# Sparse attention: the gate over the row sum goes through device memory and comes back as rows for 64 partitions a head, instead of being spread, transposed and copied

## The chip, the cores and the metric

The kernel runs on one core of one Trainium2 chip. The metric is the device time of one execution in microseconds (us); lower is better. The time of the kernel before is the median of three runs.

## What is computed

Two transformer-like blocks are computed for one sequence of 512 tokens and a model width of 1024, in float32. The change lies in the second layer of the second block, in its sparse attention with 16 query heads of width 64 over 4 key/value heads. Every query token attends in three branches, and a gate per token, head and branch weighs them:

```python
p_cmp = masked_softmax(s, ...)                      # branch 0: 32 compressed blocks
o_cmp = einsum("bhgqc,bchd->bqhgd", p_cmp, v_cmp)
...
p = masked_softmax(s, (tok <= t) ...)               # branch 1: selected blocks
o_sel = einsum("bhgqnk,bhqnkd->bqhgd", p, vs)
...
p = masked_softmax(s, wmask, axis=-1)               # branch 2: window
o_win = einsum("bhgqk,bkhd->bqhgd", p, vw)
o = g[..., 0:1] * o_cmp + g[..., 1:2] * o_sel + g[..., 2:3] * o_win
```

With 512 tokens the selection takes all blocks and the window reaches over all of the past, so branches 1 and 2 are both causal attention over 512 keys, with their own keys and values. The softmax is not divided before the product with the values: `exp` leaves the row sums, and the product is scaled afterwards by gate/sum. The change is about how this factor gets from its place to where the product needs it.

## The kernel before, in words

Tokens lie in four tiles of 128 (`NT` = 4, index `i`). The weights stream through SyncE's queue and are split in a high and a low part for TensorE; most of the time goes into matrix products with 512 columns (lines 474 to 476).

The attention stage is not written in program order. Every piece of work is added to a `Board` as a step with an engine letter (P = TensorE, S = ScalarE, V = VectorE, G = GpSimd, N = none), a cost in us, the steps it comes after, a rank, and what it takes and gives back of buffers. `Board.order` plays these steps through in time: the step that can begin first goes first, equal ones by rank. The order that comes out is the order in which the instructions are issued, each engine in its own order. A step on N holds no engine in this plan; it only lets its cost pass before its successors may begin.

There are 32 items `n` = (`pr`, `br`, `hh`): 8 pairs of heads, 2 branches, 2 heads. Two items that differ only in the head make one `m` = `n` // 2, 16 in all. For every item:

- SC (`at_s`, lines 2294 to 2296): scores of the four token tiles into three banks of PSUM on TensorE.
- MX (`at_m`, line 2306): row maxima on VectorE.
- EX (`at_x`, line 2322): `exp` on ScalarE, which also leaves the row sums in the small tile `asm`, 128 tokens x (4 tiles x 2 heads).
- TR (`at_t`, line 2349) and TH (`at_h`, line 381): transposes of the `exp` results on TensorE, and copies of them on ScalarE or VectorE.

For every `m`:

- GA (`at_g`): the reciprocal of the sums on VectorE (line 2331), and one product with the gates on GpSimd (line 2334), which spreads the 8 factors of a token over 512 columns (tile x head x 64) of a tile `u`.
- DT (`at_d`, line 2341): four transposes of `u` on TensorE into a bank, so that the 64 partitions of a head all carry its factors and the 512 tokens lie along the columns.
- DC (`at_e`, line 381 with `u`): a copy of that bank back into `u`, on ScalarE or VectorE.
- PV (`at_v`, line 2381): the product with the values on TensorE, 16 matmuls.
- U (`at_u`, line 2396): the product of PV's bank with `u`, on VectorE. It comes after DC and PV.
- For the second branch: PW (line 2388, the compressed branch), UC (line 2399), UA (line 2403), OH (line 381 with `oT`) and OL (line 2415), which add the three branches and split the sum for the output projection (steps D, lines 474 to 476 with `oT`).

GpSimd also has in this stage: the rotary steps QR (lines 1955 to 1958), some products of the compressed branch (line 2243), and at its end four loads of `h` from device memory (line 2505). The queries are turned for the scores by steps ST (line 2176). Elsewhere GpSimd's queue issues the DMAs of lines 1357 (`acsd`, 64 rows of 2 KB out of SBUF into device memory) and 1434 (`selh`, 32 runs of 512 bytes back out of `acsd`). The DMAs of lines 1881 to 1885 (`pe`, `w`, `rope`: 128 rows of 128 bytes, 1 KB and 512 bytes) are issued by ScalarE's queue.

Of the kernel before, what the change touches and what calls it, by code (L numbers as in the profile page):

```python
# [12 lines left out]
F32 = mybir.dt.float32  # L13
# [3 lines left out]
ALU = mybir.AluOpType  # L17
AX = mybir.AxisListType

P = 128  # L20
T = 512
D = 1024
NT = 4
# [317 lines left out]
def kernel(ctx: ExitStack, tc: tile.TileContext, ins, out):  # L341
    nc = tc.nc
    mm = nc.tensor.matmul
    V, S, G = nc.vector, nc.scalar, nc.gpsimd
# [11 lines left out]
    def nm(s):  # L356
        uid[0] += 1
        return f"{s}_{uid[0]}"
# [4 lines left out]
    def st(shape=(P, 512), dt=F32, name="s"):  # L363
        return bp.tile(list(shape), dt, name=nm(name), tag="s", bufs=NS)

    def bank(name="b"):
        return pp.tile([P, 512], F32, name=nm(name), tag="b", bufs=8)
# [12 lines left out]
    def copy(eng, o, a):  # L380
        S.copy(o, a) if eng == "S" else V.tensor_copy(o, a)
# [11 lines left out]
    ident = cp.tile([P, P], F32, name="ident")  # L393
# [266 lines left out]

    h = [None] * NT
    hsp = tc.dram_tile([T, D], F32, name="hsp")
    modc = cp.tile([P, 112], F32, name="modc")
    modp = [None]
    crow = cp.tile([P, D], F32, name="crow")
# [152 lines left out]
    for q in range(4):  # L818
        r = wp.tile([P, 1024], F32, name=f"xraw{q}", tag="raw", bufs=NRAW)
# [745 lines left out]
    kts = [None] * 16  # L1565
# [135 lines left out]
    for g in range(4):  # L1701
        steps = scan_steps(g)
        if g:
            q = Gr[g - 1]
# [21 lines left out]
    q = Gr[3]  # L1726
# [17 lines left out]
    kts = None  # L1744
# [226 lines left out]
    gts = kbg[:, 128:].rearrange("p (t j) -> p t j", t=NT)  # L1971
# [26 lines left out]
    B = Board(spare=ASPARE, slack=ASLACK)  # L1998
    qt = [gt(name="q") for _ in range(NT)]
    xk, Kx, Qs, wq, qb, qc, cb, pc, pcT = [], {}, {}, {}, {}, {}, {}, {}, {}  # L2000
    sb, nx, px, tb, pt, ob, db, us, sums, kts = {}, {}, {}, {}, {}, {}, {}, {}, {}, [None] * 8
    items = [(pr, hh, br) for pr in range(8) for br in range(2) for hh in range(2)]
    held = ws.n_split - ws.at
    loaded = ws.n_dma - ws.at
# [119 lines left out]
    for qr in range(4):  # L2124
        for t in range(NT):
            r = -5 if qr == 0 else QRANK[0] + QRANK[1] * (4 * qr - 4 + t)
            B.add(("Q", qr, t), "P", 2.57, lambda qr=qr, t=t: q_mm(qr, t),
                  (need(3) if qr < 2 else ["GM"] + need(8)) + ([("Q", qr, t - 1)] if t else [("Q", qr - 1, 3)] if qr else []),
                  r, take=1, give={"wh": 4, "wl": 4} if qr % 2 and t == 3 else ())
# [33 lines left out]
    for gp in range(2):  # L2163
        for br in range(2):
            r = KRANK if gp == 0 else 9 + br
            B.add(("KT", br, gp), "P", 0.44, lambda br=br, gp=gp: k_turn(br, gp), x_done + [("SC", 8 + 2 * br, 2)] if gp else [], r, take=1, short=True,
                  give={"s": 4} if gp and br else ())
# [24 lines left out]
    for pr in range(8):  # L2192
        r = 4 * pr - 3.5 if pr > 1 else -6
# [4 lines left out]
              give={"g": 4} if pr == 7 else ())  # L2198
# [60 lines left out]
    for hf in range(2):  # L2259
        r = -1 + 14 * hf  # L2260
        for tp in range(2):
            for qr in (2 * hf, 2 * hf + 1):
# [4 lines left out]
                      take={"s": 1} if qr % 2 == 0 else ())  # L2267
# [4 lines left out]
        for q in range(2):  # L2272
            B.add(("CT", hf, q), "P", 0.44, lambda hf=hf, q=q: c_turn(hf, q),
                  [("CX", hf, 0), ("CX", hf, 1)] + ([("CT", hf, 0)] if q else []), r, take=1, short=True,
                  give={"s": 2} if q else ())
# [7 lines left out]
    def at_s(n, q):  # L2283

        pr, hh, br = items[n]
        K = Kx[br, 2 * (pr // 4) + hh]
        qs = Qs[pr][:, hh]
        b = sb[n, q] = bank()
        at = 0
        for i in A_GRP[q]:  # L2290
            w = (i + 1) * P
            tl = slice(i * P, (i + 1) * P)
            o = b[:, at:at + w]
            mm(o, qs[:, tl], K[:, 1, :w], start=True, stop=False)  # L2294
            mm(o, qs[:, tl], K[:, 0, :w], start=False, stop=False)  # L2295
            mm(b[:, at + w - P:at + w], identb, camask, start=False, stop=True)  # L2296
            at += w

    def at_m(n, q):

        if n not in nx:
            nx[n] = small(4, "amx", 4)
        at = 0
        for i in A_GRP[q]:
            w = (i + 1) * P
            V.tensor_reduce(nx[n][:, i:i + 1], sb[n, q][:, at:at + w], AX.X, ALU.max, negate=True)
            at += w

    def at_x(n, q):

        if n not in px:
            if n % 2 == 0:
                sums[n // 2] = small(8, "asm", 4).rearrange("p (i h) -> p i h", h=2)
            px[n] = {}, gt(name="p"), st((P, 256), name="p")
        tiles, big, little = px[n]
        sm = sums[n // 2][:, :, n % 2]
        p = big[:, q * 512:(q + 1) * 512] if q < 2 else little
        b = sb.pop((n, q))
        at = 0
        for i in A_GRP[q]:  # L2320
            w = (i + 1) * P
            S.activation(p[:, at:at + w], b[:, at:at + w], AF.Exp, bias=nx[n][:, i:i + 1], accum_out=sm[:, i:i + 1])
            tiles[i] = p[:, at:at + w]
            at += w

    def at_g(m):

        pr, _, br = items[2 * m]
        nx.pop(2 * m), nx.pop(2 * m + 1)
        sm = sums.pop(m)  # L2330
        V.reciprocal(sm, sm)
        us[m] = st(name="u")
        gate = gts[:, :, 6 * pr:6 * pr + 6].rearrange("p i (h b) -> p i h b", b=3)[:, :, :, 1 + br:2 + br]
        G.tensor_tensor(us[m].rearrange("p (i h d) -> p i h d", i=NT, h=2), sm.unsqueeze(3).to_broadcast([P, NT, 2, 64]),
                        gate.to_broadcast([P, NT, 2, 64]), ALU.mult)

    def at_d(m):

        b = db[m] = bank()
        for i in range(NT):  # L2340
            nc.tensor.transpose(b[:, i * P:(i + 1) * P], us[m][:, i * P:(i + 1) * P], ident)

    def at_t(n, q):

# [22 lines left out]
    def KIND(n):  # L2367

        return ("raw" if items[n][1] else "wh"), ("raw" if n < NEARLY else "wl")
# [18 lines left out]
            mm(o[hh * 64:hh * 64 + 64], VB[:, pr // 4, 2 * (pr % 2) + hh], pcT[pr // 4][:, pr // 2 % 2],  # L2388
               start=True, stop=True)

    def at_e(m, eng):
        copy(eng, us[m], db.pop(m))

    def at_u(m):

        V.tensor_tensor(us[m], ob.pop(m), us[m], ALU.mult)
# [20 lines left out]
    for n, (pr, hh, br) in enumerate(items):  # L2417
        r, m = n, n // 2
        for q in range(3):
            B.add(("SC", n, q), "P", (0.52, 0.6, 0.32)[q], lambda n=n, q=q: at_s(n, q),  # L2420
                  [("SL", pr), ("K", br, pr // 4)], r + SCR, take=1,
                  give={"g": 1} if n in (3, 7) and q == 2 else {"g": 4} if n == 15 and q == 2 else ())
            B.add(("MX", n, q), "V", (0.62, 0.77, 0.37)[q], lambda n=n, q=q: at_m(n, q), [("SC", n, q)], r + MXR)
            B.add(("EX", n, q), "S", (0.87, 1.25, 0.62)[q], lambda n=n, q=q: at_x(n, q),
                  [("MX", n, q)] + ([("EX", n, 0)] if q else ["GS"]), r + EXR, take={"px": 1} if q == 0 else (), give=1)
        if hh:
            B.add(("GA", m), "G", 2.0, lambda m=m: at_g(m), [("EX", n - k, q) for k in range(2) for q in range(3)] + ["GC"],
                  r + 0.4, take={"s": 1})
        kinds = {KIND(n)[0]: 1}
        if hh == 0:  # L2430
            kinds[KIND(n)[1]] = kinds.get(KIND(n)[1], 0) + 1
        for q in range(3):
            d = [("EX", n, k) for k in range(3)]
            B.add(("TR", n, q), "P", (0.45, 0.34, 0.34)[q], lambda n=n, q=q: at_t(n, q),
                  d + ([("TR", n, q - 1)] if q else []), r - 1, take={"b": 1, **kinds} if q == 0 else 1, short=True,
                  give={"px": 1} if q == 2 else ())
            B.add(("TH", n, q), "SV", ((0.6, 0.5, 0.5)[q], (0.69, 0.56, 0.56)[q]), lambda eng, n=n, q=q: at_h(n, q, eng),
                  [("TR", n, q)] + ([("TH", n, q - 1)] if q else []) + ([("TH", n - 1, 2)] if q == 2 and hh else []),
                  r + 0.1, give=1)
        if hh:  # L2440
            back = dict(wh=1)
            for k in ("raw", KIND(n)[1]):
                back[k] = back.get(k, 0) + 1
            B.add(("PV", m), "P", 2.3, lambda m=m: at_v(m), [("TH", n - k, q) for k in range(2) for q in range(3)], r - 1,
                  take=1, short=True, give=back)
            B.add(("DT", m), "P", 0.5, lambda m=m: at_d(m), [("GA", m)], r - 0.5, take=1, short=True)
            B.add(("DC", m), "SV", (0.6, 0.69), lambda eng, m=m: at_e(m, eng), [("DT", m)], r, give=1)
            B.add(("U", m), "V", 0.72, lambda m=m: at_u(m), [("DC", m), ("PV", m)], r, give=1)
            if br:
                B.add(("PW", pr), "P", 0.9, lambda pr=pr: at_w(pr), [("U", m - 1), ("CH", pr // 4, pr // 2 % 2), "vc"],  # L2450
                      r - 1.5, take=1, short=True, give={"wl": 1} if pr == 3 else ())
                B.add(("UC", pr), "V", 0.69, lambda pr=pr: at_c(pr), [("PW", pr)], r - 0.5, give=1)
                B.add(("UA", pr), "GV", (1.3, 0.62), lambda eng, pr=pr: at_a(pr, eng), [("UC", pr), ("U", m)], r, give={"s": 1})
                B.add(("OH", pr), "SVG", (0.6, 0.4, 1.3), lambda eng, pr=pr: at_o(pr, eng), [("UA", pr)], r, take={"g": 1})
                B.add(("OL", pr), "GV", (1.3, 0.62), lambda eng, pr=pr: at_p(pr, eng), [("OH", pr)], r, give={"s": 1})
# [17 lines left out]
    for hf in range(2):  # L2473
        B.add(("gp", hf), "V", 1.6, lambda hf=hf: gr_prep(hf), [("GA", 11)] + ([("gc", 0)] if hf else []), 45,
              take={"s": 2, "g": 1 - hf})
# [22 lines left out]
    sb = tb = qt = B = None  # L2498
# [10 lines left out]
    kts = None  # L2509
# [100 lines left out]
```

## Time and profile before

| | |
|---|---|
| median of 3 runs | 2333.89 us (2333.24 to 2336.09) |
| the profiled execution's own time | 2337.24 us |
| its span in the trace | 2335.5 us |
| TensorE busy | 2271.2 us, 97% of the span |
| VectorE busy | 1444.5 us, 62% |
| ScalarE busy | 996.1 us, 43% |
| GpSimd busy | 209.3 us, 9% |
| packets under 512 bytes | 12424 of 98113 |

Busy time is summed over all instructions of an engine. A busy TensorE is not one at its peak, because the ends of its matmuls are modelled. The items of the attention run from about 1740 to 1925 us after the span's start; within that stretch the shares of the engines differ from those of the whole span.

### The profile page before, as it was taken

To read this page: it belongs to the slowest core of one execution; us is meant where nothing else is said; L and a number is where in the kernel's file an instruction comes from. 1 tells how busy PE (TensorE), PEld (TensorE's weight loads), DVE (VectorE), ACT (ScalarE), POOL (GpSimd) and SP (SyncE) were. 2 spreads that over 40 slices of the span, in tenths; PEclk is the share of its full clock that TensorE was granted. 3 is DMA by queue.
4 is the path that set the end of the run, shared out by engine and by line. 5 is a ranking of instruction groups with operands and counts; after the bars stand their busy time and mean duration, and the time that the engine had idled before them with its cause. 6 is when DMAs were issued, how large, how long until landed. Compare 5 with 4: busy or idle time off the path is not lost.

```text
span 2335.5 us, 30687 instructions
## 1 busy us (share of the span) xinstructions
PE 2271.2 (97%) x11890; PEld 1869.8 (80%) x11890; DVE 1444.5 (62%) x2411; ACT 996.1 (43%) x1697; POOL 209.3 (9%) x288
## 2 busy tenths in 40 slices
PE   8898999999999999999999999999999999999998
PEld 6676888788888887887789888888887768888887
DVE  3676666687855686776866556566757876323334
ACT  3454434342433365555535323236445765223122
POOL 0000040220000030110100000003332110000000
PEclk9998999999999999999999999999999999999999
DMA  5765523345642422221262567463420022323222
GB/s 177 201 182 149 184 87 118 126 135 193 191 148 90 130 90 76 73 76 61 74 230 88 193 191 239 147 209 106 130 55 10 19 100 91 108 73 109 90 90 72
DMA packets 98113, 286.75 MB, mean 123 GB/s; under 512 B 12424, under 2 KB 13192, under 8 KB 97968
## 3 DMA queue, kind: packets, MB, share of 16 engines
q1 hardware_dynamic: 59328, 209.02, 28.2%
q10 hardware_dynamic: 36288, 71.32, 9.2%
q0 software_dynamic: 2352, 4.46, 0.6%
q8 instruction: 93, 1.52, 0.3%
q14 instruction: 52, 0.43, 0.1%
HBM read 261.55 MB, written 8.52 MB: 116 GB/s over the span
## 4 chain that ended last, share of the span: by engine, by line
PE 73%; DVE 4%; ACT 1%; issue 1%; DMA 0%; POOL 0%; DVEq 0%; POOLq 0%; ACTq 0%
PE b L474 21%; PE b L476 21%; PE b L475 21%; PE b L2381 2%; PE b L2349 1%; PE b L2294 1%; PE b L2295 1%; PE b L1509 1%; PE b L1513 1%; DVE wl L157 0%; PE b L626 0%; DVE wl L115 0%; PE b L1474 0%; PE b L2388 0%; PE b L2296 0%
## 5 line engine op out<-in xcount | busy, mean ns | idle before, releaser
L474 PE MATMUL b<-xTl,wh 128*128 128x512 f32 (+1 forms) x1776 | 664.7, 374 | 9.5 <-DVE xTl L642 9.3
L476 PE MATMUL b<-xTh,wl 128*128 128x512 f32 (+1 forms) x1776 | 654.3, 368 | 0.5 <-DVE wl L115 0.5
L475 PE MATMUL b<-xTh,wh 128*128 128x512 f32 (+1 forms) x1776 | 654.1, 368 | 0.0
L115 DVE TENSOR_TENSOR wl<-raw,wh 128x1024 fp32r<-128x1024 f32 x317 | 388.0, 1235 | 287.2 <-ACT wh L114 286.2
L474 PEld LDWEIGHTS b<-xTl,wh 128*128 128x128 f32 x1776 | 336.8, 190 | 67.1 <-DVE xTl L642 11.6
L114 ACT CAST wh<-raw 128x1024 fp32r<-128x1024 f32 x317 | 327.3, 1049 | 142.1 <-PE b L476 66.9
L476 PEld LDWEIGHTS b<-xTh,wl 128*128 128x128 f32 x1776 | 335.9, 189 | 57.1 <-DVE wl L115 1.0
L475 PEld LDWEIGHTS b<-xTh,wh 128*128 128x128 f32 x1776 | 336.6, 190 | 54.3 <-issue 1.4
L474 PE MATMUL b<-wl,pT 128*128 128x512 f32 x520 | 202.7, 390 | 0.0
L476 PE MATMUL b<-wh,pT 128*128 128x512 f32 x520 | 202.3, 389 | 0.0
L475 PE MATMUL b<-wh,pT 128*128 128x512 f32 x520 | 202.3, 389 | 0.0
L706 DVE SCALAR_TENSOR_TENSOR mraw<-mraw,crow 128x512 f32<-128x512 f32 x224 | 145.6, 686 | 7.6 <-DMA mraw<-in_w_mod_dram 7.5
L474 PE MATMUL b<-wl,xTh 128*128 128x512 f32 (+1 forms) x352 | 127.8, 363 | 11.7 <-DVE wl L131 7.6
L476 PE MATMUL b<-wh,xTl 128*128 128x512 f32 (+1 forms) x352 | 124.8, 355 | 0.0
L475 PE MATMUL b<-wh,xTh 128*128 128x512 f32 (+1 forms) x352 | 124.7, 354 | 0.0
L476 PEld LDWEIGHTS b<-wh,pT 128*128 128x128 f32 x520 | 97.6, 188 | 20.2
L475 PEld LDWEIGHTS b<-wh,pT 128*128 128x128 f32 x520 | 97.6, 188 | 20.2
L474 PEld LDWEIGHTS b<-wl,pT 128*128 128x128 f32 x520 | 97.6, 188 | 20.1
L480 ACT CAST pT<-sa 128x512 fp32r<-128x512 f32 x44 | 27.3, 621 | 193.0 <-DVE sa L1753 193.0
L1169 ACT ACTIVATE c<-b,cols 128x512 f32<-128x512 f32 x44 | 34.4, 781 | 165.2 <-PE b L476 161.8
L1749 ACT ACTIVATE sa<-b 128x512 f32<-128x512 f32 x44 | 26.3, 598 | 162.1 <-PE b L476 159.0
L1753 DVE TENSOR_TENSOR sa<-sa,b 128x512 f32<-128x512 f32 x44 | 30.3, 688 | 88.4 <-PE b L476 88.4
(456 smaller groups left out, 3581.4 us busy)
## 6 DMA issues: line engine op xcount, KB each, us to landing
mraw<-in_w_mod_dram ACTq DMA_DIRECT2D x224, 256.0 KB, 3.7
raw<-in_w_f1u_dram SPq DMA_DIRECT2D x44, 512.0 KB, 3.7
raw<-in_w_f2u_dram SPq DMA_DIRECT2D x44, 512.0 KB, 3.7
raw<-in_w_f3u_dram SPq DMA_DIRECT2D x44, 512.0 KB, 3.7
raw<-in_w_f1d_dram SPq DMA_DIRECT2D x22, 512.0 KB, 3.6
raw<-in_w_f2d_dram SPq DMA_DIRECT2D x22, 512.0 KB, 3.6
raw<-in_w_f3d_dram SPq DMA_DIRECT2D x22, 512.0 KB, 3.6
raw<-in_w_sbqk_dram SPq DMA_DIRECT2D x16, 512.0 KB, 4.8
```

The lines of the kernel that those rows point to most:

```text
L114: self.nc.scalar.copy(h[:, :w], t[:, :w])
L115: self.nc.vector.tensor_sub(l[:, :w], t[:, :w], h[:, :w].bitcast(F32))
L474: mm(o, lh, rl, start=start, stop=False)
L475: mm(o, lh, rh, start=False, stop=False)
L476: mm(o, ll, rh, start=False, stop=stop)
L480: S.copy(h, psrc)
L706: V.scalar_tensor_tensor(r, r, 1.0, crow[:, k * 512:(k + 1) * 512], ALU.mult, ALU.mult, accum_out=modp[0][:, i % 8, k:k + 1])
L1169: S.activation(c, b, AF.Identity, bias=col("ffn_conv_b", i), scale=col("ffn_conv", 2 * 44 + i))
L1509: mm(yb[hh * 64:hh * 64 + 64, cs], self.xdt[c][:, j * P + hh * 64:j * P + hh * 64 + 64], m[:, hh, cs], start=True, stop=True)
L1749: S.activation(c, b, AF.Silu)
L1753: V.tensor_mul(c, c, b)
L2381: mm(o[hh * 64:hh * 64 + 64, s_ * P:], v32[br][:, s_, 2 * (pr // 4) + hh], w[:, :wd], start=s_ == 0, stop=s_ == NT - 1)
```

## The change

`at_g` no longer spreads the factors on GpSimd. VectorE multiplies the reciprocals by the gates (128 x 8 elements). GpSimd's queue then issues four DMAs: two write the 512 factors of each head into a row of a tile in device memory, `gsp[m]`, and two read each row into the 64 partitions of its head in `u`. The transposes (DT) and the copy out of their bank (DC) go. In the plan, GA becomes a step of 0.35 us on VectorE, and DC a step without work that lets 6.0 us pass between GA and U.

```diff
@@ tile_two_blocks_kernel
     hsp = tc.dram_tile([T, D], F32, name="hsp")
+    gsp = [tc.dram_tile([2, T], F32, name=f"gsp{m}") for m in range(16)]
@@ at_g
         V.reciprocal(sm, sm)
+        gate = gts[:, :, 6 * pr:6 * pr + 6].rearrange("p i (h b) -> p i h b", b=3)[:, :, :, br + 1]
+        V.tensor_tensor(sm, sm, gate, ALU.mult)
+        to = gsp[m]
         us[m] = st(name="u")
-        gate = gts[:, :, 6 * pr:6 * pr + 6].rearrange("p i (h b) -> p i h b", b=3)[:, :, :, 1 + br:2 + br]
-        G.tensor_tensor(us[m].rearrange("p (i h d) -> p i h d", i=NT, h=2), sm.unsqueeze(3).to_broadcast([P, NT, 2, 64]),
-                        gate.to_broadcast([P, NT, 2, 64]), ALU.mult)
-
-    def at_d(m):
-
-        b = db[m] = bank()
-        for i in range(NT):
-            nc.tensor.transpose(b[:, i * P:(i + 1) * P], us[m][:, i * P:(i + 1) * P], ident)
+        for hh in range(2):
+            G.dma_start(to[hh:hh + 1, :].rearrange("o (i q) -> q (o i)", q=P), sm[:, :, hh])
+        for hh in range(2):
+            G.dma_start(us[m][hh * 64:hh * 64 + 64], to[hh:hh + 1, :].to_broadcast([64, T]))
...
-    def at_e(m, eng):
-        copy(eng, us[m], db.pop(m))
@@ steps
-            B.add(("GA", m), "G", 2.0, lambda m=m: at_g(m), [("EX", n - k, q) for k in range(2) for q in range(3)] + ["GC"],
+            B.add(("GA", m), "V", 0.35, lambda m=m: at_g(m), [("EX", n - k, q) for k in range(2) for q in range(3)] + ["GC"],
                   r + 0.4, take={"s": 1})
...
-            B.add(("DT", m), "P", 0.5, lambda m=m: at_d(m), [("GA", m)], r - 0.5, take=1, short=True)
-            B.add(("DC", m), "SV", (0.6, 0.69), lambda eng, m=m: at_e(m, eng), [("DT", m)], r, give=1)
+            B.add(("DC", m), "N", 6.0, lambda: None, [("GA", m)], r)
             B.add(("U", m), "V", 0.72, lambda m=m: at_u(m), [("DC", m), ("PV", m)], r, give=1)
```

## Rows read from the trace of the kernel before

**Rows 1.** Busy time of each engine in one stretch of the attention.

```profile
core 0: us, PE busy (x) PEld busy (x) DVE busy (x) ACT busy (x) POOL busy (x), PEclk, DMA share, GB/s
1800.00:1900.00 100.00, 99.49 (x737) 70.62 (x738) 86.94 (x186) 73.16 (x229) 12.59 (x12) 1.00 0.10 27
```

**Rows 2.** Chain that ended last, 1720 to 1945 us: start, us, what.

```profile
1766.41 0.44 PE b L2341 x4
...
1776.67 0.44 PE b L2176 x4
...
1916.62 0.44 PE b L2341 x4
```

**Rows 3.** Groups by line, 1740 to 1930 us: busy, mean ns, idle before.

```profile
L2334 POOL TENSOR_TENSOR u<-asm,kbg 128x512 f32<-128x512 f32 x16 | 16.8, 1047 | 120.2 <-DVE asm L2331 113.5 <-PE b L2296 6.7
...
L2396 DVE TENSOR_TENSOR u<-b,u 128x512 f32<-128x512 f32 x16 | 11.1, 691 | 14.7 <-PE b L2381 14.6
L2341 PE MATMUL b<-ident,u 128*128 128x128 f32 x64 | 9.7, 274 | 0.0
...
L381 ACT COPY u<-b 128x512 f32<-128x512 f32 x9 | 5.3, 590 | 3.3 <-PE b L2341 3.1
...
L381 DVE COPY u<-b 128x512 f32<-128x512 f32 x7 | 4.8, 687 | 1.8 <-PE b L2341 1.8
...
L2239 DVE TENSOR_TENSOR csm<-csm,kbg 128x16 f32<-128x16 f32 x3 | 0.5, 179 | 0.1
```

**Rows 4.** VectorE in order of time: reciprocal (GA) and U of one m.

```profile
1777.01 0.19 DVE L2331 RECIPROCAL asm<-asm 128x8 f32<-128x8 f32 x1
1786.27 0.69 DVE L2396 TENSOR_TENSOR u<-b,u 128x512 f32<-128x512 f32 x1
...
1788.61 0.18 DVE L2331 RECIPROCAL asm<-asm 128x8 f32<-128x8 f32 x1
...
1796.95 0.69 DVE L2396 TENSOR_TENSOR u<-b,u 128x512 f32<-128x512 f32 x1
...
1828.44 0.20 DVE L2331 RECIPROCAL asm<-asm 128x8 f32<-128x8 f32 x1
...
1834.60 0.69 DVE L2396 TENSOR_TENSOR u<-b,u 128x512 f32<-128x512 f32 x1 [1.53 <-PE b L2381]
...
1895.22 0.19 DVE L2331 RECIPROCAL asm<-asm 128x8 f32<-128x8 f32 x1
...
1902.35 0.69 DVE L2396 TENSOR_TENSOR u<-b,u 128x512 f32<-128x512 f32 x1 [1.15 <-PE b L2381]
```

**Rows 5.** GpSimd in order of time, three stretches.

```profile
886.78 0.77 POOL L1357 DMA_DIRECT2D acsd<-acsr  x1 [37.21 <-DVE acsr L1356]
889.92 1.26 POOL L1434 DMA_DIRECT2D selh<-acsd  x2 [2.37 <-DMA acsd<-acsr]
...
1765.02 0.32 POOL L1958 TENSOR_TENSOR q<-q,ta 128x64 f32<-128x64 f32 x1
...
1828.81 1.04 POOL L2334 TENSOR_TENSOR u<-asm,kbg 128x512 f32<-128x512 f32 x1 [7.34 <-DVE asm L2331]
```

**Rows 6.** DMA issues (count, KB, median us to landing), and one line's landing.

```profile
acsd<-acsr POOLq DMA_DIRECT2D x1, 128.0 KB, 2.5
...
DMA to landing us min/median/max: 2.3/2.5/3.8
```

**Rows 7.** Instructions on tile h from 1905 us: ns min/median/max, first, last.

```profile
L1665 DVE SCALAR_TENSOR_TENSOR h<-yg,rs,h x8: 741/744/748, 1944.0 to 1968.7; 128x512 f32<-128x512 f32 x8
...
L2505 POOL DMA_DIRECT2D h<-hsp x4: 540/546/612, 1911.2 to 1912.9; - x4
```

**Rows 8.** Busy time by stretch; the last two columns are DMA share and GB/s.

```profile
888.00:888.50 0.50, 0.50 (x7) 0.38 (x7) 0.00 (x0) 0.50 (x3) 0.00 (x0) 1.00 1.00 221
888.50:889.00 0.50, 0.50 (x9) 0.50 (x7) 0.00 (x0) 0.50 (x1) 0.00 (x0) 1.00 0.18 41
...
1631.00:1632.00 1.00, 1.00 (x6) 0.84 (x5) 0.00 (x0) 0.66 (x2) 1.00 (x4) 1.00 0.31 87
1632.00:1633.00 1.00, 1.00 (x7) 0.79 (x7) 0.35 (x1) 1.00 (x2) 1.00 (x3) 1.00 0.40 126
```

More of the change, by code (lines that the diff above doesn't have):

```diff
@@ L2000 @@
     xk, Kx, Qs, wq, qb, qc, cb, pc, pcT = [], {}, {}, {}, {}, {}, {}, {}, {}
-    sb, nx, px, tb, pt, ob, db, us, sums, kts = {}, {}, {}, {}, {}, {}, {}, {}, {}, [None] * 8
+    sb, nx, px, tb, pt, ob, us, sums, kts = {}, {}, {}, {}, {}, {}, {}, {}, [None] * 8
     items = [(pr, hh, br) for pr in range(8) for br in range(2) for hh in range(2)]
```

## The prediction

> **What bounds the kernel now.** I read the shares of the stage first, since those of the whole span mix stages with other limits. From 1800 to 1900 us TensorE is busy for 99.5 us of 100, VectorE for 86.9, ScalarE for 73.2 and GpSimd for 12.6 [rows 1]. So TensorE sets the pace, and VectorE is so full that a wait in its queue has little idle time to disappear in. The chain of waits comes next: the transposes of line 2341 lie on it, 0.44 us for each group of four, from m0 to m15 [rows 2]; 14 of the 16 groups stand there. The groups by line give what the change removes, and say that GpSimd idles 120 us ahead of its 16 products, nearly all of it waiting for VectorE's reciprocal [rows 3]: before the change GpSimd's queue is free when a gate is ready. Last, VectorE in order of time shows the distance that this change lives or dies by: from the start of the reciprocal to the start of U, the instruction that needs the spread factor [rows 4]. For m2 to m13, twelve pairs of which the first (1788.61 to 1796.95, 8.34 us) and the last (1895.22 to 1902.35, 7.13 us) are shown, it is 88.3 us in all, 7.36 on average, the shortest 6.16 (m6). The other four are longer; the shortest of these is m1 with 9.26.
>
> **What it removes.** TensorE: 16 groups of 0.44 us on the chain, 7.0 us [rows 2]. That is the whole possible gain: TensorE sets the pace, and the other things removed, nine copies of 590 ns on ScalarE, seven of 687 on VectorE and 16 products on GpSimd [rows 3], lie beside it. VectorE gets a product of 128x8; the nearest row, 128x16, takes 179 ns [rows 3], so 16 of them are 2.9 us against 4.8 us of copies that leave: VectorE becomes no fuller. As the copies may have gone to either engine, I count nothing for this.
>
> **What it adds: a round trip.** U no longer waits for a chain of engines but for four DMAs in a row on GpSimd's queue: write, write, read, read. A read can't be issued before its write has landed. Step by step, from the start of the reciprocal:
> - Reciprocal 0.2, product 0.2, and the hand-over to GpSimd of 0.2 (reciprocal 1828.44 + 0.20, GpSimd begins at 1828.81) [rows 3 to 5]: the first write is issued at 0.6.
> - An issue holds GpSimd for 0.63 (two in 1.26) or 0.77 [rows 5]. These have 32 and 64 runs; a write here has 512 runs of 4 bytes, since neither side has two neighbouring elements in order. No row shows such a transfer. Below, the issue grows by nothing (four of `h`, with 128 rows each, take 546 ns [rows 7]). Above, that row's time grows with the runs, 0.546 x 512/128 = 2.2 us. I take 0.62, since from 32 to 128 runs it doesn't grow. The second write has been issued at 1.84.
> - The data of `acsd` begin 1.2 us after its issue began (886.78; DMA engines still idle before 888.0), 0.45 after the issue ended, and use all 16 engines for 0.59 us for 64 rows [rows 5, 8]: 147 ns for a row on an engine. The three loads at 1631 use 0.71 us x 16 engines for 384 rows of 128 to 1024 bytes [rows 8]: 30 ns for a row. 512 elements over 16 engines are 32 on each: 0.95 us at 30 ns, 4.7 us at 147, and nothing if they overlap wholly. By size the 30 is nearer, by direction (into device memory) the 147; I take 50 ns, an estimate nearer to the former, 1.6 us for a write. The two share the engines: 1.22 + 0.45 + 2 x 1.6 = 4.9.
> - Landing: `acsd` landed 2.5 us after its issue [rows 6], so at 889.28, 0.7 after its last data; the next issue came 0.64 later (889.92) [rows 5]. The second read is issued at 4.9 + 0.7 + 0.64 = 6.2; the first read has gone before, when the first write had landed.
> - A read lands 2.5 us after its issue (line 1434: 2.3 to 3.8; `acsd`, as many bytes as here, 2.5) [rows 6]: 8.7, and VectorE begins at 8.8.
>
> The lower end is a write that costs no more than that of `acsd`: from its issue to the next 3.14 us (886.78 to 889.92) [rows 5], 0.6 + 0.62 + 3.14 + 2.5 + 0.1 = 7.0. The upper end of all bounds together, 2.2 us an issue and 4.7 a write, is about 16.6.
>
> **What the round trip meets.** The plan lets U come 6.0 us after GA. With 0.35 for GA and two planner lags of 0.13 that is 6.6 after the reciprocal began, and where PV is later, PV decides; so I expect U to stand in VectorE's queue about where it stands now, 7.36 us behind. If the data come later, VectorE waits, and behind U in its queue stand the row maxima of the next items and copies of transposes: ScalarE's `exp` waits for the maxima and TensorE for both. The next GA comes behind U on VectorE, so the next round trip starts late too: nothing is made up, and the stalls add. The sum for m2 to m13 is 12 x (8.8 - 7.36) = 17.3 us. In these the transposes' saving is used up, since it only brings U nearer to its GA. For m0, m1, m14 and m15 the round trip is hidden and the saving stays, 4 x 0.44 = 1.8. Net +15.5. Against the profiled execution's own time, 2337.2, that is 2352.7; the median of the runs is 3.4 lower, so **2349 us**.
>
> **What stays hidden.** GpSimd is held by the waiting reads for some 6 us after each gate. Behind them stand: the rotary products after the first gate (the last begins at 1765.02, and the turned queries are next used on the chain at 1776.67, 11 us of cover [rows 2, 5]), the products of line 2243, and the four loads of `h`, issued at 1911.2 and first used at 1944.0, over 30 us of cover [rows 7]. I count nothing; without the cover each would cost at most those 6 us, once. Other transfers are few in the stage (DMA share 0.10 [rows 1]).
>
> The Trainium skill, "DMA: Bandwidth & Descriptors", section "Rules for kernel authors", speaks against the change: an access whose last dimension is strided becomes one descriptor per element. No row here shows such a transfer; by that page the writes have 1024 elements to process for each m, and the terms above between 30 and 147 ns are what is then open.
>
> **Rivals.**
> 1. The round trip is hidden (faster). If the elements overlap in the engines it takes 7.0 us, and U's place or a PV that comes late covers it; from 6.9 down (7.36 less 0.44) all of the 7.0 us is gained: 2326.9. For it: the lower end is met by rows of the same queue, and DMA engines are idle in the stage. Against it: the writes have eight times the runs of `acsd`. It decides at 7.1, where the gain falls below 0.2%. Chance 0.20. The Trainium skill, "DMA: Bandwidth & Descriptors", section "Anatomy of one DMA", puts one DMA from this queue at about 2.0 us plus bytes at 436 GB/s; two in a row after 1.2 us would give about 5.5 us, an estimate from that page, and this rival. The trace disagrees in part: 2.5 us to landing and 0.64 to the next issue.
> 2. Gain and stall cancel: 7.1 to 7.9 us. At 7.5, 12 x 0.14 = 1.7 against 1.8: 2334. Chance 0.13.
> 3. The forecast's mechanism: 7.9 to 10.7 us. At 10.7, 12 x 3.34 + 1.4 for m1 (9.26), less 1.3 for the other three: +40. So 2339 to 2374, this case's own range. Chance 0.42.
> 4. The elements are dear: 10.7 us or more, GpSimd's issue growing with the runs (2.2 us each alone: 5.0 + 0.45 + 1.6 + 0.7 + 0.64 + 2.5 + 0.1 = 11.0, about 2377) or the DMA engines near 147 ns. At 12.5: 12 x 5.14 + 3.2 - 1.3 = +64, 2397. For it: nothing in the trace bounds a 4-byte element better. Against it: issue times don't grow from 32 to 128 runs. Chance 0.25.
>
> **How the numbers follow.** 0.2% of the median, 4.7 us, is about what a measurement can tell from no change. Faster is rival 1, 0.20; same rival 2, 0.13; slower the other two, 0.67. The range runs from 2327, the full gain, which only a reordering by chance could pass, to 2397; above lies some 0.1, the dearer part of rival 4, and a little lies below.
>
> **What would show it.** In the profile of the changed kernel: no transposes from `u`; 64 more issues on GpSimd's queue; some 16,000 more packets under 512 bytes if each element is one. The write's issue time and its landing decide the terms: 0.62 and about 4 us. U's idle time on VectorE should be put down to a DMA into `u`, some 1 to 2 us each time, and the distance from reciprocal to U be near 8.8 for m2 to m13. The stage of 1800 to 1900 should last longer with TensorE less than 99% busy. If U still waits for PV and not for the DMA, rival 1 holds. What would make this wrong: a plan that puts U farther from GA than 6.6 us, other work that the new order brings between them, or an element cost outside of 30 to 60 ns.

## The result and the profile after

The changed kernel is slower: 2446.28 us (median of 4 runs, 2445.02 to 2447.64) against 2334.99 us (four runs as well), a ratio of 1.0474 with a 95% interval of 1.0461 to 1.0487. The profiled execution took 2447.64 us with a span of 2445.9. The forecast was 2349 with a range up to 2397.

The 111 us are lost in the attention. From the reciprocal of m1 to U of m15 it is 257.9 us (1781.64 to 2039.58), where the kernel before took 146.4 (1777.01 [rows 4] to 1923.44). VectorE's instructions before, with the reciprocal of m15 first, and after:

```profile
1909.91 0.20 DVE L2331 RECIPROCAL asm<-asm 128x8 f32<-128x8 f32 x1
...
1923.44 0.69 DVE L2396 TENSOR_TENSOR u<-b,u 128x512 f32<-128x512 f32 x1 [4.63 <-PE b L2381]
```

```profile
1781.64 0.19 DVE L2332 RECIPROCAL asm<-asm 128x8 f32<-128x8 f32 x1
...
2039.58 0.69 DVE L2392 TENSOR_TENSOR u<-b,u 128x512 f32<-128x512 f32 x1 [8.88 <-DMA u<-gsp]
```

The busy times by stretch, for the stage of [rows 1] and the one after it:

```profile
core 0: us, PE busy (x) PEld busy (x) DVE busy (x) ACT busy (x) POOL busy (x), PEclk, DMA share, GB/s
...
1800.00:1900.00 100.00, 66.83 (x407) 44.62 (x406) 50.12 (x112) 44.58 (x140) 16.80 (x25) 0.82 0.13 26
1900.00:2000.00 100.00, 65.31 (x377) 43.90 (x377) 45.19 (x104) 39.58 (x126) 15.78 (x24) 0.79 0.23 32
```

TensorE falls from 99.5 us to 66.8, and from 737 matmuls in the 100 us to 407; no engine is full any more. The granted clock falls from 1.00 to 0.82. So somebody waits. The waits from 1740 to 2040 us (us in total, times, longest) say who:

```profile
DVE u L2392 <- DMA u<-gsp: 121.9, 14, 14.5
PEld b L2295 <- DVE u L2392: 57.4, 8, 12.4
ACT p L2323 <- DVE amx L2307: 56.7, 16, 11.5
PE b L2295 <- DVE u L2392: 55.5, 8, 12.2
```

Line 2392 is U (2396 in [rows 3], where it waited for PV's bank for 14.6 us in all). Now it waits for the DMA into `u`, 121.9 us in 14 of 16 cases, and the next scores on TensorE and the `exp` on ScalarE wait behind it, as the prediction had it. The two kinds of DMA, by their lines (ns min/median/max, first and last start), and the landing of the first:

```profile
L2338 POOL DMA_DIRECT2D gsp<-asm x32: 762/783/853, 1747.3 to 2022.6; - x32
...
DMA to landing us min/median/max: 8.7/9.5/11.7
```

```profile
u<-gsp POOLq DMA_DIRECT2D x32, 128.0 KB, 4.1
...
gsp<-asm POOLq DMA_DIRECT2D x32, 2.0 KB, 9.5
```

A write of 2 KB lands 9.5 us after its issue; `acsd`, 64 times as many bytes, took 2.5 [rows 6]. The issue itself holds GpSimd for 0.78 us only. One m in order of time, m7, on VectorE and on GpSimd:

```profile
1886.13 0.19 DVE L2332 RECIPROCAL asm<-asm 128x8 f32<-128x8 f32 x1
1886.36 0.17 DVE L2334 TENSOR_TENSOR asm<-asm,kbg 128x8 f32<-128x8 f32 x1
...
1901.58 0.69 DVE L2392 TENSOR_TENSOR u<-b,u 128x512 f32<-128x512 f32 x1 [6.40 <-DMA u<-gsp]
```

```profile
1887.08 1.55 POOL L2338 DMA_DIRECT2D gsp<-asm  x2 [5.11 <-DVE amx L2307]
1896.55 0.55 POOL L2340 DMA_DIRECT2D u<-gsp  x1 [7.92 <-PE b L2348]
1897.61 0.54 POOL L2340 DMA_DIRECT2D u<-gsp  x1 [0.52 <-DMA gsp<-asm]
```

The profile puts the wait of the first read down to TensorE (line 2348); the landing of the first write, 9.5 us after 1887.08, falls on the same moment, and the experiments below decide between the two.

And the same stretch in half microseconds; the last two columns are the DMA engines' share and GB/s:

```profile
1888.50:1889.00 0.50, 0.50 (x4) 0.50 (x3) 0.47 (x1) 0.00 (x0) 0.13 (x1) 0.50 0.36 4
1889.00:1889.50 0.50, 0.50 (x5) 0.50 (x3) 0.49 (x1) 0.39 (x2) 0.00 (x0) 0.50 0.36 4
1889.50:1890.00 0.50, 0.50 (x3) 0.24 (x2) 0.49 (x2) 0.50 (x4) 0.00 (x0) 0.92 0.01 0
1890.00:1890.50 0.50, 0.50 (x6) 0.49 (x6) 0.47 (x2) 0.42 (x2) 0.00 (x0) 1.00 0.00 0
...
1896.00:1896.50 0.50, 0.50 (x7) 0.50 (x6) 0.00 (x0) 0.37 (x2) 0.00 (x0) 1.00 0.00 0
...
1899.50:1900.00 0.50, 0.00 (x0) 0.00 (x0) 0.00 (x0) 0.00 (x0) 0.00 (x0) 0.83 1.13 221
1900.00:1900.50 0.50, 0.00 (x0) 0.00 (x0) 0.00 (x0) 0.00 (x0) 0.00 (x0) 0.50 0.74 123
...
1902.00:1902.50 0.50, 0.17 (x1) 0.17 (x2) 0.50 (x2) 0.00 (x0) 0.00 (x0) 0.50 0.00 0
```

What is to be seen here is an absence. The DMA engines show some activity for about 1 us, up to 1889.5, and then nothing until after the reads are issued. The first read could not go before 1896.55. For 7 us neither GpSimd nor a DMA engine shows work, while TensorE still has some (0.50 us of each 0.50 up to 1896.5), and yet the writes have not landed. The last rows also show the side effect on the clock: after TensorE has had nothing since 1897.7, the granted clock is 0.50 from 1900.0 on, its lower level of 1.2 GHz, and it is still 0.50 when the next matmuls begin (1902.33).

### The profile page after: what moved, and what is told of

Its sections match the earlier page's. It is cut to its first block, busy times and chain, and to the rows that moved or that the text cites. A ratio compares the mean times of both kernels' runs of the same rounds, so it can differ in the third digit from the quotient of the medians.

```text
span 2445.9 us, 30651 instructions
## 1 busy us (share of the span) xinstructions
PE 2294.6 (94%) x11826; PEld 1882.1 (77%) x11826; DVE 1439.5 (59%) x2418; ACT 992.0 (41%) x1691; POOL 234.6 (10%) x335
## 2 busy tenths in 40 slices
DMA packets 100674, 291.02 MB, mean 119 GB/s; under 512 B 13960, under 2 KB 14728, under 8 KB 100528
## 4 chain that ended last, share of the span: by engine, by line
PE 66%; DMA 5%; issue 4%; DVE 4%; ACT 1%; POOL 1%; DVEq 0%; POOLq 0%; ACTq 0%
PE b L474 20%; PE b L476 20%; PE b L475 20%; DMA gsp<-asm 2%; DMA u<-gsp 2%; PE b L1510 1%; PE b L1514 0%; PE b L2380 0%; PE b L626 0%; PE b L2295 0%; DVE wl L115 0%; PE b L2348 0%; PE b L1475 0%; DVE wl L157 0%; PE b L1464 0%
## 5 line engine op out<-in xcount | busy, mean ns | idle before, releaser
L474 PEld LDWEIGHTS b<-xTl,wh 128*128 128x128 f32 x1776 | 336.9, 190 | 67.1 <-DVE xTl L642 11.6
L474 PE MATMUL b<-wl,xTh 128*128 128x512 f32 (+1 forms) x352 | 128.1, 364 | 11.4 <-DVE wl L131 8.0
L2323 ACT ACTIVATE p<-b,amx 128x256 f32<-128x256 f32 (+3 forms) x128 | 66.6, 532 | 58.9 <-DVE amx L2307 56.7
```

Of the source, the lines that this page charges most:

```text
L474: mm(o, lh, rl, start=start, stop=False)
```

## The experiments

The theory after this reading: the writes' landing makes the loss, and it is set by what happens to 4-byte elements in device memory. Its rivals: the new order of steps costs by itself; GpSimd's queue makes the transfers slow; the elements are slow one by one, wherever they go.

**No trip, same order.** The DMAs are left out, and GpSimd spreads the factor with an instruction of the same shape as before (an addition, so the values mean nothing); nothing is transposed or copied.

```diff
-        to = gsp[m]
...
-        for hh in range(2):
-            G.dma_start(to[hh:hh + 1, :].rearrange("o (i q) -> q (o i)", q=P), sm[:, :, hh])
-        for hh in range(2):
-            G.dma_start(us[m][hh * 64:hh * 64 + 64], to[hh:hh + 1, :].to_broadcast([64, T]))
+        G.tensor_tensor(us[m].rearrange("p (i h d) -> p i h d", i=NT, h=2), sm.unsqueeze(3).to_broadcast([P, NT, 2, 64]),
+                        sm.unsqueeze(3).to_broadcast([P, NT, 2, 64]), ALU.add)
```

> This kernel keeps the changed order of steps but leaves the four DMAs out: GpSimd spreads the factor into u as before, and it is neither transposed nor copied, so the factors stand in the wrong places. If the loss is the wait for the round trip, the full saving of the transposes is seen: 16 x 0.44 = 7.0 us less than before, 2322 to 2331. If the loss comes from the new order of steps, or from the banks and copies that the plan now lacks, it stays: 2340 or more.

Measured: 2331.09 against 2336.11, ratio 0.9978 (0.9969 to 0.9988). The order is not at fault. With this order, 5 us are left to win if the factors came for nothing, of the 7.0 that TensorE no longer does.

**Runs of 16 bytes.** Sums and factors lie as (head, tile), so a token's four values of a head are neighbours, and they are written side by side.

```diff
-                sums[n // 2] = small(8, "asm", 4).rearrange("p (i h) -> p i h", h=2)
+                sums[n // 2] = small(8, "asm", 4).rearrange("p (h i) -> p i h", h=2)
...
-            G.dma_start(to[hh:hh + 1, :].rearrange("o (i q) -> q (o i)", q=P), sm[:, :, hh])
+            G.dma_start(to[hh:hh + 1, :].rearrange("o (q i) -> q (o i)", q=P), sm[:, :, hh])
```

> The writes have the same bytes in the same queue, but each partition's four values go out as one run of 16 bytes: 128 runs instead of 512 elements. This leaves the order of the tokens out (the rows come back permuted). If the number of elements sets the 9.5 us from issue to landing, it falls to about 2.5 + 7/4 = 4.3 us and the time to about 2375 (distance from reciprocal to U near 11 us). If it is a price of this queue or of writing from SBUF into device memory whatever the shape, landing stays at 8.5 to 9.5 us and the time at 2446.

Measured: 2335.27 in one run, landing 1.7 us (count, KB, median us to landing):

```profile
gsp<-asm POOLq DMA_DIRECT2D x32, 2.0 KB, 1.7
```

The loss is gone, more than was expected. Landing fell by more than the number of runs did (9.5/4 would still be 2.4, with nothing fixed in it), so a price for each element is not enough as an explanation.

**Elements apart.** The number of elements stays, only their distance in device memory changes. The four kernels differ in one number; their first lines fill the rows that are read back, ahead of the stage. Here for 512 bytes:

```diff
-    gsp = [tc.dram_tile([2, T], F32, name=f"gsp{m}") for m in range(16)]
+    gsp = [tc.dram_tile([2, T * P], F32, name=f"gsp{m}") for m in range(16)]
+    for m in range(16):
+        G.dma_start(gsp[m][:, :T], ins["ln_g"][0:2, :T])
...
-            G.dma_start(to[hh:hh + 1, :].rearrange("o (i q) -> q (o i)", q=P), sm[:, :, hh])
+            G.dma_start(to[hh:hh + 1, :].rearrange("o (i q s) -> q (o i) s", q=P, s=P)[:, :, 0], sm[:, :, hh])
...
-            G.dma_start(us[m][hh * 64:hh * 64 + 64], to[hh:hh + 1, :].to_broadcast([64, T]))
+            G.dma_start(us[m][hh * 64:hh * 64 + 64], to[hh:hh + 1, :T].to_broadcast([64, T]))
```

> The same 512 elements for each write, but each 512 bytes from the next in device memory instead of 4; the rows read back are other, initialised values, so the result's order is left out. If neighbouring elements wait for each other because they fall into one line of device memory, landing falls to 3 to 5 us and the time to 2370 or less. If each element costs by itself, wherever it lands, landing stays at 8.5 to 10 us and the time at 2440 or more.

> As the run with the elements 512 bytes apart, but 64 bytes apart; the result's order is left out again. If elements wait for each other only within some 64 bytes of device memory, landing stays near 2.3 us and the time at 2331 to 2337. If the unit is larger (512 bytes), eight elements still share one and landing is 3 us or more; with 128 elements to a unit it was 9.5.

> Elements 32 bytes apart; the result's order is left out. If a unit of 32 bytes is what elements share, each has its own and the writes land at 2.2 us, as at 64 and 512 bytes. If the unit is 64 bytes, two share one and landing lies between 2.2 and the 3.0 us of 16 bytes apart, about 2.5.

> Elements 16 bytes apart. If the unit is 64 bytes, four elements share one instead of sixteen: landing about 2.3 + 7.2 x 3/15 = 3.7 us, time 2335 to 2350. If the unit is 32 bytes, two share one instead of eight: 2.3 + 7.2/7 = 3.3 us. If the sharing of memory units is not the cause, and only the reach of 2 KB, landing is near 9 us, as at 4 bytes apart.

In all four the rows read back are not the factors in order. One run each:

| distance of elements | elements in 32 bytes | landing of a write, us (median) | time, us |
|---|---|---|---|
| 512 bytes | 1 | 2.3 | 2333.58 |
| 64 bytes | 1 | 2.2 | 2335.72 |
| 32 bytes | 1 | 2.2 | 2329.40 |
| 16 bytes | 2 | 3.0 | 2345.37 |
| 4 bytes (the change) | 8 | 9.5 | 2446.28 |

The DMA issues of the kernel with 16 bytes and of that with 32 (count, KB, median us to landing):

```profile
gsp<-asm POOLq DMA_DIRECT2D x32, 2.0 KB, 3.0
```

```profile
gsp<-asm POOLq DMA_DIRECT2D x32, 2.0 KB, 2.2
```

The same 512 elements, from the same queue, with the same issue time of 0.78 us, land in 2.2 to 2.3 us as long as each has 32 bytes of device memory to itself. With two in 32 bytes it is 0.8 us more, with eight 7.3: some 1 us for each further element in the same 32 bytes. Shown is that the closeness of the elements in device memory makes the late landing: their number, their place in SBUF and the queue are the same in all five rows. That they wait for neighbours in one unit of 32 bytes fits the five rows, but is not shown, because the reach of a write grows with the distance (2, 8, 16 KB and more). The reach alone is not it: the runs of 16 bytes stay within 2 KB and land in 1.7 us. These also put two writes into each 32 bytes, though a quarter as many in all, so the price for each neighbour holds for the 512 elements only. What the memory does with such a write is not shown by any run. Even 0.8 us is felt: with 16 bytes U waited 31.5 us for its DMA (us in total, times, longest).

```profile
DVE u L2394 <- DMA u<-gsp: 31.5, 12, 6.0
```

**SyncE's queue.** All four DMAs go from `nc.sync` instead of GpSimd.

> The same four DMAs, issued from SyncE's queue instead of GpSimd's. If GpSimd's making of the transfers sets the landing, it falls to 3 to 5 us for the writes and the time to 2350 to 2380. If the elements set it in the DMA engines or at device memory, landing stays at 8 us or more and the time within 15 us of 2446.

Measured: 2430.89 in one run. The profile gives 15.7 us (12.3 to 19.2) from a write's issue to its landing here, but the reads that wait for the writes were issued sooner. SyncE's queue in order of time (m1), and what it waited for in the stage:

```profile
1778.05 0.92 SPq L2338 DMA_DIRECT2D gsp<-asm  x2
1786.55 2.26 SPq L2340 DMA_DIRECT2D u<-gsp  x2
```

```profile
SPq L2340 <- DMA gsp<-asm: 146.4, 23, 11.3
```

From the first write of an m to its first read it is 7.4 to 12.3 us, 9.5 in the median of the 16; in the changed kernel, counted in the same way, 9.1 to 11.8, 10.0 in the median. So the 15.7 can't be the landing that the reads waited for, and that landing is about the same from either queue: it is not GpSimd's making of the transfers. It is 15 us less than the changed kernel all the same. The trip of m1 is 1.1 us shorter (14.35 from reciprocal to U instead of 15.46): its first write goes 0.46 us after the reciprocal began and not 0.95, and both issues take 0.92 and not 1.56. The rest was not taken apart.

**U later.** The plan lets 16 us pass instead of 6.0.

```diff
-            B.add(("DC", m), "N", 6.0, lambda: None, [("GA", m)], r)
+            B.add(("DC", m), "N", 16.0, lambda: None, [("GA", m)], r)
```

> The changed kernel with the plan's step DC at 16 us instead of 6.0, so that U stands behind the round trip of some 15.5 us. If only the place of U in VectorE's queue is wrong, its idle time there goes and the time falls to 2331 to 2340. If GpSimd's queue, held for 10.9 us by the DMAs of one m (1.55 for the writes, some 8.2 of waiting, 1.07 for the reads) against 9.5 us between two gates before, becomes the pace, 14 x 1.4 = 20 us remain: about 2350. If the stalls have another cause than the round trip, the time stays at 2430 or more.

Measured: 2380.13 in one run. Some 66 us come back, but not to the 2350 expected of the held queue. GpSimd in order of time shows the new pace:

```profile
1828.73 1.55 POOL L2338 DMA_DIRECT2D gsp<-asm  x2
1839.50 1.07 POOL L2340 DMA_DIRECT2D u<-gsp  x2 [9.22 <-PE b L2387]
1840.57 1.55 POOL L2338 DMA_DIRECT2D gsp<-asm  x2
...
1862.06 1.07 POOL L2340 DMA_DIRECT2D u<-gsp  x2 [9.15 <-PE b L2297]
1863.12 1.55 POOL L2338 DMA_DIRECT2D gsp<-asm  x2
```

The queue runs end to end: write, wait, read, and at once the next write, 11.5 us for each m (1828.73 to 1863.12, three of them). The gates before came every 9.5 us (m1 to m15, 1777.01 to 1909.91, 14 steps). U still waited 49.3 us. So the trip as it is can't be hidden by a later U: it is longer than the period of the work it serves, in one queue that takes one m at a time. That it is 2380 and not 2350 is to be seen on VectorE (reciprocals of m1 and m15, U of m15):

```profile
1778.94 0.19 DVE L2332 RECIPROCAL asm<-asm 128x8 f32<-128x8 f32 x1
...
1946.61 0.19 DVE L2332 RECIPROCAL asm<-asm 128x8 f32<-128x8 f32 x1
...
1971.70 0.69 DVE L2392 TENSOR_TENSOR u<-b,u 128x512 f32<-128x512 f32 x1 [17.36 <-DMA u<-gsp]
```

From m1's reciprocal to m15's it is 34.8 us longer than before, 28 of them from the queue's pace (14 x 2.0). The last U comes 25.09 us behind its reciprocal instead of 13.53, 11.6 more. Together 46 us, near the 44 above the kernel before; where the other 7 of the 34.8 come from was not taken apart.

**Runs of 16 bytes with the whole result.** `u` keeps its columns as (token, tile), and U, UC, OH and OL read or write with a stride of 16 bytes.

```diff
+    def qi(v):
+        return v.rearrange("p (q i) -> p i q", i=NT)
+    def iq(v):
+        return v.rearrange("p (i q) -> p i q", i=NT)
...
-        V.tensor_tensor(us[m], ob.pop(m), us[m], ALU.mult)
+        V.tensor_tensor(qi(us[m]), iq(ob.pop(m)), qi(us[m]), ALU.mult)
...
-        V.tensor_add(us[2 * pr], us[2 * pr], cb.pop(("o", pr)))
+        V.tensor_add(qi(us[2 * pr]), qi(us[2 * pr]), iq(cb.pop(("o", pr))))
...
```

> The writes in runs of 16 bytes, and u kept with its columns in the order (token, tile) until the sum is split, so that the result is the whole one: U, UC, OH and OL read or write with a stride. If landing at 1.7 us hides the round trip and the strides cost nothing on VectorE and ScalarE, the saving of the transposes is left: 2329 to 2334, a ratio of 0.996 to 0.999. If strided operands are slower (690 ns for U grows, or the copies of 0.42 us become 0.7), VectorE stalls TensorE and it is 2335 to 2345.

Measured: 2338.80 against 2335.65, ratio 1.0015 (1.0006 to 1.0024). The second case: the groups by line, 1740 to 1930 us, show the strides' price on VectorE, 1104 ns for U, where it was 691 [rows 3].

```profile
L2398 DVE TENSOR_TENSOR u<-b,u 128x512 f32<-128x512 f32 x16 | 17.7, 1104 | 9.6 <-PE b L2386 5.1 <-DMA u<-gsp 4.5
L2401 DVE TENSOR_TENSOR u<-u,b 128x512 f32<-128x512 f32 x8 | 8.9, 1110 | 2.6 <-PE b L2393 2.5
...
L2417 DVE TENSOR_TENSOR oT<-u,oT 128x512 fp32r<-128x512 f32 x8 | 8.8, 1096 | 0.4 <-ACT oT L381 0.3
```

16 x 0.41 + 8 x 0.42 + 8 x 0.41 (OL against 685 ns with the elements 64 bytes apart) are some 13 us more on the engine that has the least room after TensorE.

**Rows turned on the way out.** Two kernels turn the 128 x 8 factors before they leave, so that what is written are long runs in the natural order. The first uses one small transpose on TensorE, the second a block transpose on VectorE.

```diff
+        nc.tensor.transpose(b[:8, :P], sm.rearrange("p i h -> p h i"), ident)
...
+        copy(eng, o[:8], db.pop(m)[:8, :P])
...
+        nc.sync.dma_start(to.rearrange("h (i q) -> (h i) q", q=P), o[:8])
+        for hh in range(2):
+            nc.sync.dma_start(us[m][hh * 64:hh * 64 + 64], to[hh:hh + 1, :].to_broadcast([64, T]))
```

> The 128 x 8 factors are turned by one transpose on TensorE (0.11 us on the chain in place of 0.44), copied as 8 rows of 128 and written as 8 runs of 512 bytes in one DMA from SyncE's queue; the rows are read back as in the changed kernel, and U stands 6.5 us behind the copy in the plan. If runs of 512 bytes land at 1.7 to 2.5 us, the trip is hidden and 16 x 0.33 = 5.3 us are saved: 2328 to 2333, 0.997 to 0.999. If the longer chain (transpose, bank, copy, two DMAs in a row) comes too late for U, VectorE shows a wait for a DMA into u of over 10 us and it is 2336 or more.

```diff
+        V.tensor_tensor(crow[:, k:k + 8].rearrange("p (h i) -> p i h", h=2), sm, gate, ALU.mult)
+        V.transpose(crow[:, k + 32:k + 64], crow[:, k:k + 32])
...
+        rows = to.rearrange("h (i q) -> (h i) q", q=P)
+        for c in range(4):
+            nc.sync.dma_start(rows[:, c * 32:c * 32 + 32], crow[c * 32:c * 32 + 8, k + 32:k + 64])
...
```

> The factors are turned in blocks of 32 x 32 on VectorE, and four DMAs of 8 runs of 128 bytes write them from SyncE's queue in the natural order, so that U needs no stride. TensorE keeps the whole saving of 7.0 us, VectorE pays some 0.2 us for each m. If the trip (four issues of 0.45, landing 2 us, two reads) stays under the 8.6 us that the plan gives it, 2327 to 2332, 0.996 to 0.998. If it doesn't, U waits for its DMA and it is 2336 or more.

Measured, against 2336.39: 2333.26, ratio 0.9988 (0.9979 to 0.9997), and 2333.49, ratio 0.9989 (0.9980 to 0.9998). Both are faster than the kernel before by some 3 us of the 5 that the first experiment left to win, with intervals that only just exclude no change; both lie a little above the times expected (up to 2333 and 2332). In the second kernel the block transpose takes 211 ns, and U waits for its DMA 3.0 us in all:

```profile
L2395 DVE TENSOR_TENSOR u<-b,u 128x512 f32<-128x512 f32 x16 | 10.9, 683 | 4.8 <-DMA u<-gsp 3.0 <-PE b L2383 1.6
L2336 DVE STREAM_TRANSPOSE crow<-crow 128x32 f32<-128x32 f32 x16 | 3.4, 211 | 0.5
```

## Why the prediction was wrong

**Right: what bounds, and what the stall does.** The transposes' saving, a U that waits in VectorE's queue and stops the maxima, the `exp` and TensorE behind it, stalls that add and are not made up: the waits after show each (121.9 us at U against 111 lost). The first experiment leaves a gain of 5 us where I had 7.0.

**Wrong: the landing of the write.** From the start of the reciprocal, as the prediction's steps had it and as m7 shows it:

| step | predicted, us | m7, us |
|---|---|---|
| first write issued | 0.6 | 0.95 |
| second write issued, to its end | 1.84 | 2.5 |
| last data in the DMA engines | 4.9 | 3.4 |
| second read issued | 6.2 | 11.5 |
| U begins | 8.8 | 15.45 |

The step that failed is "Landing: `acsd` landed 2.5 us after its issue [rows 6], so at 889.28, 0.7 after its last data". I had looked for the price of the elements in the issue and in the DMA engines' time, and took the 0.7 us after that from a write of rows of 2 KB. There the elements cost near what I took (0.78 us an issue, for 0.62) or less (last data at 3.4 us, for 4.9). The price stood behind: some 7 us in which neither GpSimd nor a DMA engine shows work, where I had 0.7. The elements apart show what made it: their closeness in device memory, which no row of before shows. The reads, too, landed in 4.1 us (median) and not in 2.5. With 15.45 in place of 8.8 the prediction's own sum gives 12 x 8.09 = 97 us for m2 to m13, 6 for m1 and 5 for m14 and m15 (12.54 and 13.53 us from reciprocal to U before): 108, close to the 111 measured.

**Wrong: nothing for GpSimd's held queue.** I counted the wait of the reads as harmless for what stands behind them. What stands behind them is also the next m's writes. In the new order, which the kernel without the trip shows too, m2 and m3, m5 and m6, m8 and m9, m11 and m12, and m14 and m15 have both gates ahead of the first U. There the queue takes them one after the other. The writes of the second wait until the reads of the first have gone: m3's first write is issued 4.0 us after its reciprocal began (1809.63 to 1813.66), those of m6, m9, m12 and m15 5.3 to 9.2 us after, and that of m7 0.95. GpSimd for m2 and m3:

```profile
1803.05 1.55 POOL L2338 DMA_DIRECT2D gsp<-asm  x2 [9.62 <-DVE asm L2334]
1812.60 1.07 POOL L2340 DMA_DIRECT2D u<-gsp  x2 [8.00 <-PE b L2348]
1813.66 1.55 POOL L2338 DMA_DIRECT2D gsp<-asm  x2
1825.19 1.07 POOL L2340 DMA_DIRECT2D u<-gsp  x2 [9.97 <-issue]
```

U of m2 began at 1824.57, 11.4 us after the second of its reads was issued (1813.13); in m7 it was 4.0. The DMA engines had moved the data of these reads by 1817.0:

```profile
1816.50:1817.00 0.50, 0.00 (x0) 0.00 (x0) 0.00 (x0) 0.00 (x0) 0.00 (x0) 1.00 0.30 70
1817.00:1817.50 0.50, 0.00 (x0) 0.00 (x0) 0.00 (x0) 0.00 (x0) 0.00 (x0) 1.00 0.00 0
```

Why they landed 7.5 us after that stays open. That m3's writes came right behind them does not explain it by itself: the reads of m5 and m11 were followed as closely, and U came 4.3 and 3.0 us after the second. So the close agreement of the sum above is in part luck. The distance from reciprocal to U for m2 to m13 is 19.0 us on average (15.3 to 23.7), with which the sum would give 140 us; in exchange the second U of each two waited less than the first. Of the clock the prediction said nothing; its mean of 0.82 in the stage belongs to the price of the stalls.

**Wrong: the choice inside the bounds.** All bounds together gave 16.6 us, by the same sum some 2459; the range stopped at 12.5. Rival 4 had the right size with a chance of 0.25, though neither of its two mechanisms, GpSimd's issue (0.78 us, not 2.2) or the DMA engines' time, was it. Rivals 1 and 2 are what the same trip does once the elements have room: 2329 to 2336 at 32 bytes and more, with the order left out, one run each, in which U still waits 8 to 9 us for its DMA in all. The Trainium skill, "DMA: Bandwidth & Descriptors", section "Anatomy of one DMA", stood behind rival 1 with some 2.0 us for a small DMA: the writes with room agree (2.2 us to landing), those of the changed kernel do not (9.5).

## What to carry to other kernels

The landing of a DMA is not the sum of its issue and its bytes: before small elements are written to device memory, look at how close together they come to lie (here 32 bytes apart cost nothing, 4 bytes apart some 7 us a write), and turn the data on the chip first (here 0.2 us) so that neighbours leave as one run. A round trip in one in-order queue has a pace as well as a length: compare its hold on the queue with the period of the work that it serves, since a later consumer hides only the length. Where no row shows the operation, keep the upper bound in the range, and ask of each row that stands in for it what it would not show.

## What the runs showed of the hardware that was not expected

- Writes of 4-byte elements into device memory landed in 2.2 us when 32 bytes or more apart, in 3.0 at 16 bytes and in 9.5 at 4 bytes; from SyncE's queue, at 4 bytes, the reads behind them waited about as long (9.5 us from the first write's issue, 10.0 from GpSimd's).
- In those 9.5 us the DMA engines show activity for about 1 us. Two reads of 128 KB, moved by 1817.0, landed only at 1824.5.
- The elements are not one packet each in the trace's count from GpSimd's queue: 13960 packets under 512 bytes against 12424 before, not some 16,000 more. From SyncE's queue there were 29832.
- An issue of 512 elements held GpSimd for 0.78 us, hardly more than one of 64 rows (0.77).
- A stride of 16 bytes in `u`, read and written, took U on VectorE from 691 to 1104 ns; a 32 x 32 block transpose of 128 x 32 takes 211 ns.
